# Encoder step on one core: the sample's small matmuls and the score products laid out over all 128 rows

## The chip, the cores and the metric

One Trainium2 chip, one of its cores. The metric is device microseconds (us) of one execution. TensorE (PE in the profile, its weight loads PEld) multiplies, VectorE (DVE), ScalarE (ACT) and GpSimd (POOL) do the elementwise work, SyncE (SP) issues most DMAs.

## The reference

One inference step of a two-layer encoder for two groups of tokens: a prompt of 512 positions and a sample of 32 with 256 cached positions. What matters here of each layer:

```python
# mixing: q, k, v, u, gv = split(rmsnorm(x) @ w_in)
s = einsum('bqhmd,bkhmd->bhmqk', q, k) * (DA_DK ** -0.5)      # 4 heads, 2 maps of 64
s = where(chunk-causal mask, s, NEG);  p = softmax(s)
a = p[:, :, 0] - lam * p[:, :, 1]
o = einsum('bhqk,bkhd->bqhd', a, v)                           # then rmsnorm, (1 - lam_init)
g_out = u * (tril(w_s) @ gv + b_s)                            # 4 groups of 128
x = x + concat(o, g_out) @ w_out
# cross-attention: 4 heads of 256 into 256 memory tokens
x = x + cross_attend(rmsnorm(x), mem_k, mem_v)
# feed-forward of 2816 with a causal convolution of width 3
x = x + conv_ffn(rmsnorm(x))
```

For the sample, k and v are the cached 256 positions and the 32 new ones. New keys, values, gate rows and convolution states are outputs too.

## The kernel before

Activations stand feature by token: x is [128, 8, 544], tokens 0 to 511 the prompt and 512 to 543 the sample. For accuracy an operand is split into a high part of type fp32r and the rest, also fp32r, and a product is three matmuls (high x high, high x low, low x high). Every weight unit is loaded (line 131), split by ScalarE (134) and VectorE (135) and used by the projections of lines 262 and 279 to 281. These are nearly all of TensorE's work.

The rest are small products, and their operands have fewer than 128 rows (partitions) in many places:

- kq_T (427) transposes a head's keys and queries (435), two maps of 64 features one above the other. For map m the own half of kT holds the high part of k, the other half its low part, and qT has the high part of q in both halves, so line 522 computes q_high x (k_high + k_low) over 128 rows. The low part of q times the high part of k is line 524, with the 64 rows of the map's own half: ql[MP[m]] and kT[MP[m], m]. do_attn (509) runs it for four query blocks and two maps per head.
- The sample's keys and queries zs have 32 rows and are transposed at 452. do_attn_sample (548) makes its scores at 554 with a stationary operand of 64 columns (two maps of 32 queries), its transposed difference of probabilities at 565 with 64 rows, and the sum with the cached and the new values at 571 and 572.
- do_gate (636) multiplies the sample's gate rows, 32 of them, at 655. x_stats (219) spreads the 32 scales of the sample at 251. do_cross_scores (809) transposes the sample's 32 rows of probabilities at 860. At the start the sample's input is transposed at 993.

sum_s (300) makes each zs: ScalarE copies one half of a PSUM tile (303), VectorE adds the other (304). Its buffers turn over with two per tag, and zs, gzs and xes share one tag.

The program is written as a stream for one core; the framework's scheduler sets the order on each engine from its own costs when the program is built, and that order is fixed at run time. Engines wait for one another on semaphores. A plain fp32 product shows as two matmuls in the trace, an fp32r one or a transpose as one.

Of the kernel before, what the change touches and what calls it, by code (L numbers as in the profile page):

```python
# [34 lines left out]
def encoder_step(ctx: ExitStack, tc: tile.TileContext, a, o):  # L35
# [183 lines left out]
    def x_stats(need_bc):  # L219
# [20 lines left out]
        dg = G("t4", [128, 4, 128], "dg")  # L240
        dgs = tiny([32, 32], "dgs")
        for t in range(4):
            vec.tensor_scalar(out=dg[:, t], in0=ident, scalar1=r[:, t:t + 1], scalar2=None, op0=ALU.mult)
        vec.tensor_scalar(out=dgs, in0=ident[0:32, 0:32], scalar1=r[0:32, 4:5], scalar2=None, op0=ALU.mult)
        rbc = cp.tile([128, T], F32, tag="rbc", name="rbc")
        for i in range(2):
            pb = psS("pbc")
            for t in range(2):
                pe.matmul(out=pb[:, 128 * t:128 * t + 128], lhsT=ones, rhs=dg[:, 2 * i + t], start=True, stop=True)
            if i == 1:  # L250
                pe.matmul(out=pb[:, 256:288], lhsT=ones[0:32], rhs=dgs, start=True, stop=True)
            act.copy(rbc[:, 256 * i:256 * i + 256 + 32 * i], pb[:, 0:256 + 32 * i])  # L252
# [47 lines left out]
    def sum_s(ps, name):  # L300
        zt = tmp([32, 256], "zt", tag="zs1", bufs=1)
        zs = tmp([32, 256], name, tag="vs" if name == "vs" else "zs", bufs=2)
        act.copy(zt, ps[32:64, 0:256])
        vec.tensor_tensor(out=zs, in0=ps[0:32, 0:256], in1=zt, op=ALU.add)  # L304
        return zs
# [4 lines left out]
    def load_consts(l):  # L310
# [52 lines left out]
        vec.tensor_scalar(out=c["nlam"], in0=c["nlam"], scalar1=-lam_init, scalar2=None, op0=ALU.add)  # L363
        c["eye"] = cp.tile([64, 32], F32, tag="eye", name="eye")
        pool.tensor_copy(c["eye"][0:32], ident[0:32, 0:32])
# [36 lines left out]
    def do_kq(l, h, ve):  # L402
        c = LC[l]
        pr, pv, prs = proj_tm(pop(f"kq{h}"))
        z = G("zr", [128, 4, 256], "z")
        sq = G("t4", [128, 4, 256], "sq")
        for i in range(2):
            act.copy(z[:, 2 * i:2 * i + 2], pv[i])
            act.activation(out=sq[:, 2 * i:2 * i + 2], in_=pv[i], func=AF.Square)
        zs = sum_s(prs, "zs")  # L410
        sqs = tmp([32, 256], "sqs", tag="zs1", bufs=1)
        act.activation(out=sqs, in_=zs, func=AF.Square)
# [9 lines left out]
        norm_rope(zs.unsqueeze(1), 32, 1, None, rs[0:32, 16:20], c, 4)  # L422
        sp.dma_start(out=o["dkp"][l, 0, :, h].rearrange("(t p) m d -> p t (m d)", p=128), in_=z[:, :, 0:128])
        sp.dma_start(out=o["dks"][l, 0, :, h].rearrange("p m d -> p (m d)"), in_=zs[:, 0:128])
        return z, zs

    def kq_T(l, h, z, zs):

        kT = G("kq", [128, 2, 512], "kT", F32R)
        qT = G("kq", [128, 2, 512], "qT", F32R)  # L430
        ql = G("p", [128, 512], "ql", F32R)
        for half in range(2):
# [3 lines left out]
            for m in range(2):  # L436
# [4 lines left out]
                else:  # L441
                    act.activation(out=qT[own, m], in_=ps[own], func=AF.Copy, scale=0.125)
                    vec.scalar_tensor_tensor(out=ql[own], in0=ps[own], scalar=0.125, in1=f32(qT[own, m]),
                                             op0=ALU.mult, op1=ALU.subtract)
# [6 lines left out]
        for half in range(2):  # L451
            pe.transpose(ps[:, 256 + 32 * half:288 + 32 * half], zs[:, 128 * half:128 * half + 128],
                         ident[0:32, 0:32])
        skq = tmp([128, 352], "skq", tag="skq", bufs=2)
        act.copy(skq[:, 0:288], ps[:, 0:288])
        for m in range(2):
            pr = slice(64 * m, 64 * m + 64)
            pool.memset(skq[pr, 320 - 32 * m:352 - 32 * m], 0.0)
            act.activation(out=skq[pr, 288 + 32 * m:320 + 32 * m], in_=ps[pr, 288:320], func=AF.Copy, scale=0.125)
        return kT, qT, ql, skq  # L460

    def do_v(l, hp, r):
# [4 lines left out]
        zs = sum_s(prs, "vs")  # L467
        vec.tensor_scalar(out=zs, in0=zs, scalar1=r[0:32, 4:5], scalar2=None, op0=ALU.mult)
        hv = 2 * hp
        sp.dma_start(out=o["dvp"][l, 0, :, hv:hv + 2].rearrange("(t p) h d -> p t (h d)", p=128), in_=vr)  # L470
        sp.dma_start(out=o["dvs"][l, 0, :, hv:hv + 2].rearrange("p h d -> p (h d)"), in_=zs)
        return [(vr[:, :, 128 * j:128 * j + 128], zs[:, 128 * j:128 * j + 128]) for j in range(2)]

# [35 lines left out]
    def do_attn(l, h, kqs, vv, og):  # L509
# [6 lines left out]
        for i in range(4):  # L516
# [6 lines left out]
            for m in range(2):  # L523
                pe.matmul(out=ps[m][:, 0:nn], lhsT=ql[MP[m], q0:q0 + 128], rhs=kT[MP[m], m, 0:nn],
                          start=False, stop=True)
                vec.memset(ps[m][0:64, n - 64:n], NEG)
# [21 lines left out]
    def do_attn_sample(l, h, kqs, vv, st):  # L548
# [4 lines left out]
        ps = psS("pSs")  # L553
        pe.matmul(out=ps[0:64, 0:288], lhsT=skq[:, 288:352], rhs=skq[:, 0:288], start=True, stop=True)
        e = G("e", [64, 320], "es")
        mx = tiny([64, 4], "mxs")
        vec.tensor_reduce(out=mx[:, 0:1], in_=ps[0:64, 0:288], axis=AX, op=ALU.max, negate=True)
        act.activation(out=e[:, 0:288], in_=ps[0:64, 0:288], func=AF.Exp, bias=mx[:, 0:1], accum_out=mx[:, 1:2])
        vec.reciprocal(out=mx[:, 2:3], in_=mx[:, 1:2])
# [43 lines left out]
    def do_gv(l, j, r):  # L603
# [7 lines left out]
        zs = sum_s(prs, "gzs")  # L611
        vec.tensor_scalar(out=zs, in0=zs, scalar1=r[0:32, 4:5], scalar2=None, op0=ALU.mult)
# [4 lines left out]
        gelu2(zs, t1s)  # L617
        z8 = z.rearrange("p t (g c) -> p (t g) c", c=128)
        zs2 = zs.rearrange("p (g c) -> p g c", c=128)
        for b in range(8):  # L620
# [10 lines left out]
        vec.tensor_tensor(out=t1s.rearrange("p (g c) -> p g c", c=128), in0=zs.rearrange("p (g c) -> p g c", c=128),  # L631
                          in1=c["gmg"][0:32].unsqueeze(1).to_broadcast([32, 2, 128]), op=ALU.mult)
# [3 lines left out]
    def do_gate(l, j, vn, zs, ws):  # L636
# [172 lines left out]
    def do_cross_scores(h, mk, cmT, qq):  # L809
# [38 lines left out]
        for dc in range(2):  # L848
            pe.matmul(out=ps[0:32, 0:256], lhsT=qs[:, dc], rhs=cmT[:, dc], start=(dc == 0), stop=(dc == 1))
        es = tmp([32, 256], "xes", tag="zs", bufs=2)  # L850
        sx = tiny([32, 4], "sxs")
        vec.tensor_reduce(out=sx[:, 0:1], in_=ps[0:32, 0:256], axis=AX, op=ALU.max)
        vec.tensor_tensor(out=sx[:, 1:2], in0=sx[:, 0:1], in1=nrq[0:32, 4:5], op=ALU.mult)
        act.activation(out=es, in_=ps[0:32, 0:256], func=AF.Exp, scale=rq[0:32, 4:5], bias=sx[:, 1:2],
                       accum_out=sx[:, 2:3])
        vec.reciprocal(out=sx[:, 3:4], in_=sx[:, 2:3])
        vec.tensor_scalar(out=es, in0=es, scalar1=sx[:, 3:4], scalar2=None, op0=ALU.mult)
        pt = psB("pxsT")
        for mc in range(2):
# [267 lines left out]
```

## Time and profile before

| | |
|---|---|
| median of 3 runs | 1704.07 us (1703.63 to 1704.73) |
| profiled execution | 1704.66 us, its span 1702.9 us |
| TensorE busy | 1683.1 us (99%), 13115 matmuls |
| VectorE, ScalarE, GpSimd busy | 1006.2 (59%), 727.5 (43%), 250.4 (15%) us |
| granted TensorE clock | 1.00 of full speed over nearly all the span |

Busy time of TensorE counts pipelined matmuls whose ends are modelled, so its share says that it has work, not that it runs at its peak; how fast it goes is read from the steps between starts.

### The profile page before, as it was taken

How to read it: one execution, taken by the hardware profiler on the slowest of the kernel's cores; microseconds unless marked ns; L12 is line 12 of the kernel's file. 1: busy time of each engine (PE TensorE's matmuls, PEld its weight loads, DVE VectorE, ACT ScalarE, POOL GpSimd, SP SyncE). 2: the span in 40 equal slices, each digit the busy share in tenths (PEclk: the TensorE clock that was granted, in tenths of full speed). 3: DMA queues.
4: the chain of work that ended last, by engine and by line, in shares of the span. 5: the costliest groups of instructions: out<-in, count | busy, mean ns of one | idle time of the engine just before them, and what ended most of it. 6: DMA issues, size and time to landing. Idle time of an engine off the chain costs nothing.

```text
span 1702.9 us, 32510 instructions
## 1 busy us (share of the span) xinstructions
PE 1683.1 (99%) x13115; PEld 1623.8 (95%) x13115; DVE 1006.2 (59%) x2218; ACT 727.5 (43%) x1481; POOL 250.4 (15%) x676
## 2 busy tenths in 40 slices
PE   7999999999999999999999999999999999999998
PEld 6988899999999999999998888999999999999998
DVE  6778765565476634665367677555555765256642
ACT  5456754454333312333345576545543333133321
POOL 3000014221211000110111000332222110001100
PEclk9999999999999999999999999999999999999999
DMA  6222133442223233223342222243332323333141
GB/s 185 81 87 72 64 103 101 137 131 90 88 75 94 70 87 111 87 69 88 94 121 68 76 70 79 87 131 112 117 95 75 93 64 88 101 93 99 55 119 55
DMA packets 200988, 158.03 MB, mean 93 GB/s; under 512 B 8670, under 2 KB 200038, under 8 KB 200838
## 3 DMA queue, kind: packets, MB, share of 16 engines
q1 hardware_dynamic: 200774, 155.82, 30.0%
q8 instruction: 103, 1.69, 0.4%
q14 instruction: 47, 0.39, 0.1%
q10 hardware_dynamic: 64, 0.14, 0.0%
HBM read 144.83 MB, written 11.10 MB: 92 GB/s over the span
## 4 chain that ended last, share of the span: by engine, by line
PE 95%; ACT 1%; DVE 1%; SPq 1%; POOL 1%; DMA 0%; issue 0%; ACTq 0%
PE pfda L262 8%; PE pfua L262 8%; PE pfga L262 8%; PE pfdb L262 8%; PE pfub L262 8%; PE pfgb L262 8%; PE pr L281 4%; PE pr L279 4%; PE pr L280 4%; PE pwob L262 3%; PE pwoa L262 3%; PE pwca L262 3%; PE pqb L262 3%; PE pqa L262 3%; PE pwcb L262 3%; PE pm L281 2%
## 5 line engine op out<-in xcount | busy, mean ns | idle before, releaser
L135 DVE TENSOR_TENSOR hl<-raw,hl 128x1024 fp32r<-128x1024 f32 (+2 forms) x280 | 316.6, 1132 | 256.7 <-ACT hl L134 256.1
L134 ACT CAST hl<-raw 128x1024 fp32r<-128x1024 f32 (+2 forms) x280 | 269.9, 964 | 403.5 <-PE pfdb L262 137.6
L262 PE MATMUL pfda<-at,hl 128*128 128x272 f32 x1056 | 266.6, 289 | 0.0
L262 PE MATMUL pfdb<-at,hl 128*128 128x272 f32 x1056 | 266.3, 288 | 0.0
L262 PE MATMUL pfga<-hx,hl 128*128 128x272 f32 x1056 | 263.8, 287 | 0.0
L262 PE MATMUL pfgb<-hx,hl 128*128 128x272 f32 x1056 | 263.7, 287 | 0.0
L262 PE MATMUL pfua<-hx,hl 128*128 128x272 f32 x1056 | 259.3, 287 | 0.5 <-ACT rbc L252 0.5
L262 PE MATMUL pfub<-hx,hl 128*128 128x272 f32 x1056 | 259.1, 287 | 0.0
L262 PEld LDWEIGHTS pfda<-at,hl 128*128 128x128 f32 x1056 | 199.2, 189 | 0.0
L262 PEld LDWEIGHTS pfdb<-at,hl 128*128 128x128 f32 x1056 | 198.7, 188 | 0.1
L262 PEld LDWEIGHTS pfga<-hx,hl 128*128 128x128 f32 x1056 | 198.5, 188 | 0.0
L262 PEld LDWEIGHTS pfgb<-hx,hl 128*128 128x128 f32 x1056 | 198.4, 188 | 0.0
L262 PEld LDWEIGHTS pfua<-hx,hl 128*128 128x128 f32 x1056 | 196.2, 188 | 0.7 <-ACT rbc L252 0.7
L262 PEld LDWEIGHTS pfub<-hx,hl 128*128 128x128 f32 x1056 | 196.2, 188 | 0.0
L280 PE MATMUL pr<-hl,hx 128*128 128x256 f32 x512 | 147.0, 288 | 2.7 <-DVE hl L135 2.7
L279 PE MATMUL pr<-hl,hx 128*128 128x256 f32 x512 | 146.8, 287 | 1.4 <-DVE vs L304 0.9
L281 PE MATMUL pr<-hl,hx 128*128 128x256 f32 x512 | 147.7, 289 | 0.1
L280 PEld LDWEIGHTS pr<-hl,hx 128*128 128x128 f32 x512 | 97.1, 190 | 5.7 <-DVE hl L135 3.2
L279 PEld LDWEIGHTS pr<-hl,hx 128*128 128x128 f32 x512 | 98.0, 192 | 4.0 <-DVE vs L304 1.1
L281 PEld LDWEIGHTS pr<-hl,hx 128*128 128x128 f32 x512 | 96.9, 190 | 3.3 <-issue 1.4
L262 PE MATMUL pwcb<-co,hl 128*128 128x272 f32 x384 | 87.1, 288 | 0.0
L262 PE MATMUL pwca<-co,hl 128*128 128x272 f32 x384 | 86.9, 289 | 0.0
(358 smaller groups left out, 3330.0 us busy)
## 6 DMA issues: line engine op xcount, KB each, us to landing
raw<-in_w_up_dram SPq DMA_DIRECT2D x80, 512.0 KB
raw<-in_w_down_dram SPq DMA_DIRECT2D x32, 512.0 KB
raw<-in_w_in_dram SPq DMA_DIRECT2D x24, 512.0 KB
raw<-in_w_in_dram SPq DMA_DIRECT2D x32, 256.0 KB
raw<-in_w_out_dram SPq DMA_DIRECT2D x32, 256.0 KB
raw<-in_wq_c_dram SPq DMA_DIRECT2D x16, 512.0 KB
raw<-in_wk_c_dram SPq DMA_DIRECT2D x16, 512.0 KB
raw<-in_wv_c_dram SPq DMA_DIRECT2D x16, 512.0 KB
```

The source lines that it names most:

```text
L134: act.copy(hl[:, 0, 0:n * wc], raw[:, 0:n * wc])
L135: vec.tensor_tensor(out=hl[:, 1, 0:n * wc], in0=raw[:, 0:n * wc], in1=f32(hl[:, 0, 0:n * wc]), op=ALU.subtract)
L262: pe.matmul(out=ps[0 if n0 == 0 else 1][:, 0:nn], lhsT=hl[:, wpart, kk, col * 128:col * 128 + 128], rhs=mv[:, n0:n0 + nn], start=first and ...
L279: pe.matmul(out=out, lhsT=lh(k), rhs=hl[:, 0, k % 4], start=(k == 0), stop=False)
L280: pe.matmul(out=out, lhsT=lh(k), rhs=hl[:, 1, k % 4], start=False, stop=False)
L281: pe.matmul(out=out, lhsT=ll(k), rhs=hl[:, 0, k % 4], start=False, stop=(k == k8 - 1))
```

## The change

Every small product named above, except those of lines 571, 572, 582 and the narrow statistics, gets operands of 128 rows, with zeros where there was nothing:

- ql becomes [128, 2, 512]; the half that isn't the map's own is set to zero by GpSimd, and line 524 multiplies all 128 rows.
- zs, gzs, vs and xes become [128, 256] tiles that GpSimd sets to zero before their first 32 rows are written; their transposes and products take all 128 rows, and a transpose writes 128 columns where it wrote 32.
- skq puts the queries first, and line 554 takes columns 0 to 127 as its stationary operand: 64 columns of queries and 64 of cached keys, whose scores nobody reads. The softmax of the sample runs over 128 partitions. eye is zero below row 64, so line 565 multiplies 128 rows, of which 64 count.
- dgs and the input tile xins get 128 rows; xins is set to zero by VectorE before its DMA.

```diff
-        dgs = tiny([32, 32], "dgs")
+        dgs = tiny([128, 32], "dgs")
...
-                pe.matmul(out=pb[:, 256:288], lhsT=ones[0:32], rhs=dgs, start=True, stop=True)
+                pe.matmul(out=pb[:, 256:288], lhsT=ones, rhs=dgs, start=True, stop=True)
...
-        zs = tmp([32, 256], name, tag="vs" if name == "vs" else "zs", bufs=2)
+        zs = tmp([128, 256], name, tag="vs" if name == "vs" else "zs", bufs=2)
+        pool.memset(zs, 0.0)
         act.copy(zt, ps[32:64, 0:256])
-        vec.tensor_tensor(out=zs, in0=ps[0:32, 0:256], in1=zt, op=ALU.add)
+        vec.tensor_tensor(out=zs[0:32], in0=ps[0:32, 0:256], in1=zt, op=ALU.add)
...
-        c["eye"] = cp.tile([64, 32], F32, tag="eye", name="eye")
+        c["eye"] = cp.tile([128, 32], F32, tag="eye", name="eye")
+        pool.memset(c["eye"], 0.0)
...
-        ql = G("p", [128, 512], "ql", F32R)
+        ql = G("p", [128, 2, 512], "ql", F32R)
+        for m in range(2):
+            pool.memset(f32(ql[MP[1 - m], m]), 0.0)
...
-            pe.transpose(ps[:, 256 + 32 * half:288 + 32 * half], zs[:, 128 * half:128 * half + 128],
-                         ident[0:32, 0:32])
+            pe.transpose(ps[:, 256 + 128 * half:384 + 128 * half], zs[:, 128 * half:128 * half + 128], ident)
...
-                pe.matmul(out=ps[m][:, 0:nn], lhsT=ql[MP[m], q0:q0 + 128], rhs=kT[MP[m], m, 0:nn],
+                pe.matmul(out=ps[m][:, 0:nn], lhsT=ql[:, m, q0:q0 + 128], rhs=kT[:, m, 0:nn],
                           start=False, stop=True)
...
-        pe.matmul(out=ps[0:64, 0:288], lhsT=skq[:, 288:352], rhs=skq[:, 0:288], start=True, stop=True)
-        e = G("e", [64, 320], "es")
+        pe.matmul(out=ps[:, 0:288], lhsT=skq[:, 0:128], rhs=skq[:, 64:352], start=True, stop=True)
+        e = G("e", [128, 320], "es")
...
-            pe.matmul(out=pgs[:, 32 * jj:32 * jj + 32], lhsT=zs[:, 128 * jj:128 * jj + 128], rhs=ws[0:32, g, 0:32],
+            pe.matmul(out=pgs[:, 32 * jj:32 * jj + 32], lhsT=zs[:, 128 * jj:128 * jj + 128], rhs=ws[:, g, 0:32],
...
-        es = tmp([32, 256], "xes", tag="zs", bufs=2)
+        es = tmp([128, 256], "xes", tag="zs", bufs=2)
+        pool.memset(es, 0.0)
...
-            pe.transpose(pt[:, 32 * mc:32 * mc + 32], es[:, 128 * mc:128 * mc + 128], ident[0:32, 0:32])
+            pe.transpose(pt[:, 128 * mc:128 * mc + 128], es[:, 128 * mc:128 * mc + 128], ident)
...
-    xs = G("zr", [32, 1024], "xins")
-    act.dma_start(out=xs, in_=a["x_sample"][0])
+    xs = G("zr", [128, 1024], "xins")
+    vec.memset(xs, 0.0)
+    act.dma_start(out=xs[0:32], in_=a["x_sample"][0])
...
-        pe.transpose(ps[1][:, 256:288], xs[:, 128 * kt:128 * kt + 128], ident[0:32, 0:32])
+        pe.transpose(ps[1][:, 256:384], xs[:, 128 * kt:128 * kt + 128], ident)
```

How the built order stands, first on TensorE at the transposes of head 0 in layer 0 (ptr are the prompt's, ptrs the cached keys' and the sample's). Before:

```order
L296 MATMUL prs<-hl,xsm 64x256 x16
L435 MATMUL ptr<-ident,z 128x128 x8
L450 MATMUL ptrs<-ident,ck 128x128 x2
L452 MATMUL ptrs<-ident,zs 128x32 x2
L279 MATMUL pr<-hl,hx 128x256
```

Now:

```order
L296 MATMUL prs<-hl,xsm 64x256 x16
L439 MATMUL ptr<-ident,z 128x128 x8
L454 MATMUL ptrs<-ident,ck 128x128 x2
L456 MATMUL ptrs<-ident,zs 128x128 x2
L279 MATMUL pr<-hl,hx 128x256
```

The sequence is the same (line numbers are a few higher), and the sample's transposes write 128 columns. On TensorE at the first scores of head 0 (pS are the scores, pr the projection of a later head). Before:

```order
L279 MATMUL pr<-hl,hx 128x256
L522 MATMUL pS<-kT,qT 128x256
L524 MATMUL pS<-kT,ql 128x256
L280 MATMUL pr<-hl,hx 128x256
L281 MATMUL pr<-hl,hx 128x256
```

Now:

```order
L281 MATMUL pr<-hl,hx 128x256
L525 MATMUL pS<-kT,qT 128x256
L279 MATMUL pr<-hl,hx 128x256
L527 MATMUL pS<-kT,ql 128x256
L280 MATMUL pr<-hl,hx 128x256
```

One projection matmul now stands between the two score products; elsewhere the kinds of matmuls follow each other as before but for a few neighbours. On GpSimd at the copies that make qT of head 0 (s are the sums of a softmax). Before:

```order
L458 MEMSET skq 64x32
L458 MEMSET skq 64x32 [waits Pool_49]
L445 CAST qT<-qT 64x512 [waits Activation_49] x2
L529 COPY s_682<-sm 128x1 [waits Activation_49,Pool_49]
L529 COPY s_682<-sm 128x1 [waits Activation_49] x2
```

Now:

```order
L461 MEMSET skq 64x32
L461 MEMSET skq 64x32 [waits Pool_49]
L449 CAST qT<-qT 64x512 [waits Activation_49]
L303 MEMSET zs 128x256 [waits DVE_49,DMAHW5_49,PE_49,Pool_49]
L449 CAST qT<-qT 64x512 [waits Activation_49]
L532 COPY s_688<-sm 128x1 [waits Activation_49,Pool_49]
```

The memset of a later zs stands between the two copies and waits for VectorE, TensorE and a DMA. GpSimd has 42 memsets more than before in all.

## Rows read from the trace of the kernel before

**Rows 1.** The page's busy times: us, share of the span, instructions.
```profile
PE 1683.1 (99%) x13115; PEld 1623.8 (95%) x13115; DVE 1006.2 (59%) x2218; ACT 727.5 (43%) x1481; POOL 250.4 (15%) x676
```
**Rows 2.** The chain that ended last, shares of the span by engine.
```profile
PE 95%; ACT 1%; DVE 1%; SPq 1%; POOL 1%; DMA 0%; issue 0%; ACTq 0%
```
**Rows 3.** TensorE's waits: waiting <- waited for: us in total, times, longest.
```profile
PE pxina L991 <- DMA xin<-in_x_prompt_dram: 5.8, 1, 5.8
PE pr L280 <- DVE hl L135: 2.7, 2, 2.4
PE pxsT L860 <- DVE pT L175: 1.3, 2, 0.7
PE pwob L262 <- DVE s L647: 1.2, 2, 0.6
```
**Rows 4.** Groups by form on TensorE: count, busy us, mean ns, idle before.
```profile
L822 PE MATMUL pxS<-mkT,xq 128*128 128x256 f32 x192 | 28.9, 288 | 0.0
...
L524 PE MATMUL pS<-kT,ql 64*128 64x256 f32 x32 | 12.2, 381 | 0.0
```
**Rows 5.** Timeline of TensorE, a score product: start us, us, instruction.
```profile
62.33 0.28 PE L281 MATMUL pr<-hl,hx 128*128 128x256 f32 x1
62.45 0.28 PE L522 MATMUL pS<-kT,qT 128*128 128x256 f32 x1
62.66 0.38 PE L524 MATMUL pS<-kT,ql 64*128 64x256 f32 x1
62.98 0.39 PE L279 MATMUL pr<-hl,hx 128*128 128x256 f32 x1
63.20 0.28 PE L280 MATMUL pr<-hl,hx 128*128 128x256 f32 x1
```
**Rows 6.** Timeline of TensorE, two score products side by side.
```profile
189.16 0.62 PE L522 MATMUL pS<-kT,qT 128*128 128x384 f32 x2
189.71 0.44 PE L524 MATMUL pS<-kT,ql 64*128 64x384 f32 x2
190.08 0.68 PE L296 MATMUL prs<-hl,xsm 128*64 128x256 f32 x4
```
**Rows 7.** Timeline of TensorE, the sample's probabilities between transposes.
```profile
107.88 0.27 PE L543 MATMUL poT<-ident,ot 128*128 128x128 f32 x1
108.09 0.40 PE L565 MATMUL paTs<-es 64*128 64x32 f32 x2
108.42 0.33 PE L543 MATMUL poT<-ident,ot 128*128 128x128 f32 x1
```
**Rows 8.** Timeline of TensorE, the sample's scores.
```profile
84.56 0.28 PE L279 MATMUL pr<-hl,hx 128*128 128x256 f32 x1
84.77 0.70 PE L554 MATMUL pSs<-skq 128*64 128x288 f32 x2
85.40 0.39 PE L280 MATMUL pr<-hl,hx 128*128 128x256 f32 x1
```
**Rows 9.** Timeline of TensorE, the sample's transposes.
```profile
110.85 0.38 PE L450 MATMUL ptrs<-ident,ck 128*128 128x128 f32 x2
111.16 0.30 PE L452 MATMUL ptrs<-ident,zs 32*128 32x32 f32 x2
111.40 0.44 PE L522 MATMUL pS<-kT,qT 128*128 128x384 f32 x1
```
**Rows 10.** Timeline of SyncE, GpSimd and TensorE before head 0's first scores.
```profile
52.49 1.05 SPq L424 DMA_DIRECT2D out_dks_dram<-zs  x1
...
55.12 0.68 POOL L445 CAST qT<-qT 64x512 fp32r<-64x512 f32 x1 [10.90 <-ACT qT L442]
58.08 0.61 POOL L445 CAST qT<-qT 64x512 fp32r<-64x512 f32 x1 [2.27 <-ACT qT L442]
...
59.11 0.28 PE L522 MATMUL pS<-kT,qT 128*128 128x256 f32 x1
```
**Rows 11.** Groups by form on VectorE: count, busy us, mean ns, idle before.
```profile
L74 DVE MEMSET ones<- 128x128 f32 x1 | 0.2, 165 | 0.9 <-PEq L1114 0.9
```

More of the change, by code (lines that the diff above doesn't have):

```diff
@@ L240, in x_stats @@
         dg = G("t4", [128, 4, 128], "dg")
-        dgs = tiny([32, 32], "dgs")
+        dgs = tiny([128, 32], "dgs")
         for t in range(4):
             vec.tensor_scalar(out=dg[:, t], in0=ident, scalar1=r[:, t:t + 1], scalar2=None, op0=ALU.mult)
-        vec.tensor_scalar(out=dgs, in0=ident[0:32, 0:32], scalar1=r[0:32, 4:5], scalar2=None, op0=ALU.mult)
+        vec.tensor_scalar(out=dgs, in0=ident[:, 0:32], scalar1=r[:, 4:5], scalar2=None, op0=ALU.mult)
         rbc = cp.tile([128, T], F32, tag="rbc", name="rbc")
@@ L411, in do_kq @@
         sqs = tmp([32, 256], "sqs", tag="zs1", bufs=1)
-        act.activation(out=sqs, in_=zs, func=AF.Square)
+        act.activation(out=sqs, in_=zs[0:32], func=AF.Square)
         ss = tiny([128, 20], "ss")
@@ L421, in do_kq @@
         norm_rope(z, 128, 4, None, rs[:, 0:16], c, 0)
-        norm_rope(zs.unsqueeze(1), 32, 1, None, rs[0:32, 16:20], c, 4)
+        norm_rope(zs[0:32].unsqueeze(1), 32, 1, None, rs[0:32, 16:20], c, 4)
         sp.dma_start(out=o["dkp"][l, 0, :, h].rearrange("(t p) m d -> p t (m d)", p=128), in_=z[:, :, 0:128])
-        sp.dma_start(out=o["dks"][l, 0, :, h].rearrange("p m d -> p (m d)"), in_=zs[:, 0:128])
+        sp.dma_start(out=o["dks"][l, 0, :, h].rearrange("p m d -> p (m d)"), in_=zs[0:32, 0:128])
         return z, zs
@@ L442, in kq_T @@
                     act.activation(out=qT[own, m], in_=ps[own], func=AF.Copy, scale=0.125)
-                    vec.scalar_tensor_tensor(out=ql[own], in0=ps[own], scalar=0.125, in1=f32(qT[own, m]),
+                    vec.scalar_tensor_tensor(out=ql[own, m], in0=ps[own], scalar=0.125, in1=f32(qT[own, m]),
                                              op0=ALU.mult, op1=ALU.subtract)
@@ L451, in kq_T @@
         for half in range(2):
-            pe.transpose(ps[:, 256 + 32 * half:288 + 32 * half], zs[:, 128 * half:128 * half + 128],
-                         ident[0:32, 0:32])
+            pe.transpose(ps[:, 256 + 128 * half:384 + 128 * half], zs[:, 128 * half:128 * half + 128], ident)
         skq = tmp([128, 352], "skq", tag="skq", bufs=2)
-        act.copy(skq[:, 0:288], ps[:, 0:288])
+        act.copy(skq[:, 64:352], ps[:, 0:288])
         for m in range(2):
             pr = slice(64 * m, 64 * m + 64)
-            pool.memset(skq[pr, 320 - 32 * m:352 - 32 * m], 0.0)
-            act.activation(out=skq[pr, 288 + 32 * m:320 + 32 * m], in_=ps[pr, 288:320], func=AF.Copy, scale=0.125)
+            pool.memset(skq[pr, 32 - 32 * m:64 - 32 * m], 0.0)
+            act.activation(out=skq[pr, 32 * m:32 + 32 * m], in_=ps[pr, 384:416], func=AF.Copy, scale=0.125)
         return kT, qT, ql, skq
@@ L467, in do_v @@
         zs = sum_s(prs, "vs")
-        vec.tensor_scalar(out=zs, in0=zs, scalar1=r[0:32, 4:5], scalar2=None, op0=ALU.mult)
+        vec.tensor_scalar(out=zs[0:32], in0=zs[0:32], scalar1=r[0:32, 4:5], scalar2=None, op0=ALU.mult)
         hv = 2 * hp
         sp.dma_start(out=o["dvp"][l, 0, :, hv:hv + 2].rearrange("(t p) h d -> p t (h d)", p=128), in_=vr)
-        sp.dma_start(out=o["dvs"][l, 0, :, hv:hv + 2].rearrange("p h d -> p (h d)"), in_=zs)
-        return [(vr[:, :, 128 * j:128 * j + 128], zs[:, 128 * j:128 * j + 128]) for j in range(2)]
+        sp.dma_start(out=o["dvs"][l, 0, :, hv:hv + 2].rearrange("p h d -> p (h d)"), in_=zs[0:32])
+        return [(vr[:, :, 128 * j:128 * j + 128], zs[0:32, 128 * j:128 * j + 128]) for j in range(2)]
     def softmax_diff(ps, p, n, e, c, name):
@@ L553, in do_attn_sample @@
         ps = psS("pSs")
-        pe.matmul(out=ps[0:64, 0:288], lhsT=skq[:, 288:352], rhs=skq[:, 0:288], start=True, stop=True)
-        e = G("e", [64, 320], "es")
-        mx = tiny([64, 4], "mxs")
-        vec.tensor_reduce(out=mx[:, 0:1], in_=ps[0:64, 0:288], axis=AX, op=ALU.max, negate=True)
-        act.activation(out=e[:, 0:288], in_=ps[0:64, 0:288], func=AF.Exp, bias=mx[:, 0:1], accum_out=mx[:, 1:2])
+        pe.matmul(out=ps[:, 0:288], lhsT=skq[:, 0:128], rhs=skq[:, 64:352], start=True, stop=True)
+        e = G("e", [128, 320], "es")
+        mx = tiny([128, 4], "mxs")
+        vec.tensor_reduce(out=mx[:, 0:1], in_=ps[:, 0:288], axis=AX, op=ALU.max, negate=True)
+        act.activation(out=e[:, 0:288], in_=ps[:, 0:288], func=AF.Exp, bias=mx[:, 0:1], accum_out=mx[:, 1:2])
         vec.reciprocal(out=mx[:, 2:3], in_=mx[:, 1:2])
@@ L611, in do_gv @@
         zs = sum_s(prs, "gzs")
-        vec.tensor_scalar(out=zs, in0=zs, scalar1=r[0:32, 4:5], scalar2=None, op0=ALU.mult)
+        vec.tensor_scalar(out=zs[0:32], in0=zs[0:32], scalar1=r[0:32, 4:5], scalar2=None, op0=ALU.mult)
         t1s = tmp([32, 256], "gts", tag="zs1", bufs=1)
@@ L616, in do_gv @@
         gelu2(z, t1)
-        gelu2(zs, t1s)
+        gelu2(zs[0:32], t1s)
         z8 = z.rearrange("p t (g c) -> p (t g) c", c=128)
-        zs2 = zs.rearrange("p (g c) -> p g c", c=128)
+        zs2 = zs[0:32].rearrange("p (g c) -> p g c", c=128)
         for b in range(8):
@@ L630, in do_gv @@
         vec.tensor_tensor(out=zs2, in0=zs2, in1=rs[0:32, 8:10].unsqueeze(2).to_broadcast([32, 2, 128]), op=ALU.mult)
-        vec.tensor_tensor(out=t1s.rearrange("p (g c) -> p g c", c=128), in0=zs.rearrange("p (g c) -> p g c", c=128),
+        vec.tensor_tensor(out=t1s.rearrange("p (g c) -> p g c", c=128), in0=zs2,
                           in1=c["gmg"][0:32].unsqueeze(1).to_broadcast([32, 2, 128]), op=ALU.mult)
@@ L853, in do_cross_scores @@
         vec.tensor_tensor(out=sx[:, 1:2], in0=sx[:, 0:1], in1=nrq[0:32, 4:5], op=ALU.mult)
-        act.activation(out=es, in_=ps[0:32, 0:256], func=AF.Exp, scale=rq[0:32, 4:5], bias=sx[:, 1:2],
+        act.activation(out=es[0:32], in_=ps[0:32, 0:256], func=AF.Exp, scale=rq[0:32, 4:5], bias=sx[:, 1:2],
                        accum_out=sx[:, 2:3])
         vec.reciprocal(out=sx[:, 3:4], in_=sx[:, 2:3])
-        vec.tensor_scalar(out=es, in0=es, scalar1=sx[:, 3:4], scalar2=None, op0=ALU.mult)
+        vec.tensor_scalar(out=es[0:32], in0=es[0:32], scalar1=sx[:, 3:4], scalar2=None, op0=ALU.mult)
         pt = psB("pxsT")
         for mc in range(2):
-            pe.transpose(pt[:, 32 * mc:32 * mc + 32], es[:, 128 * mc:128 * mc + 128], ident[0:32, 0:32])
+            pe.transpose(pt[:, 128 * mc:128 * mc + 128], es[:, 128 * mc:128 * mc + 128], ident)
         pTs = tmp([128, 2, 32], "pTs", tag="aTs", bufs=1)
-        vec.tensor_copy(pTs, pt[:, 0:64].rearrange("p (m t) -> p m t", m=2))
+        vec.tensor_copy(pTs, pt[:, 0:256].rearrange("p (m t) -> p m t", m=2)[:, :, 0:32])
         return pT, pTs
```

## The prediction

> **What bounds the kernel.** I read the busy times first, then TensorE's waits, then the timeline of TensorE around the matmuls that the change touches, where the step from one start to the next counts and not the modelled duration. TensorE is busy 99% of the span and every other engine below 60% [rows 1], and 95% of the chain that ended last is TensorE's [rows 2]. What it waits for by name is little: 5.8 us for the first input, 2.7 for weights in the first 30 us, some 1 us each at a handful of other places [rows 3]. So a step that TensorE saves is time saved, unless the saving only brings it earlier to one of these waits.
>
> The steps show where TensorE loses time without waiting for anybody. In a plain stream a 256-column matmul starts 0.12 us after the one before (62.33 to 62.45 in [rows 5]). Around the score matmul of line 524, whose operands have 64 rows, it doesn't: 0.21 us from the L522 ahead to L524, 0.32 from L524 to the next, 0.22 to the one after, 0.75 for three steps where 0.36 is usual. The excess is **0.39 us for one matmul**. The stretched steps lie at the change from 128 rows to 64 and back. A control supports that it is the row count: line 822 also issues 256-column products that add low parts into the same sum, with 128 rows, and its 192 matmuls take 0.288 us each where the 32 of L524 take 0.381 [rows 4].
>
> **The change, part by part.** TensorE keeps its number of instructions and, by the order shown above, its sequence but for a few neighbours; what changes is the shape of eight kinds of them. I price each by the excess steps that disappear.
>
> Scores (L524): two layers of four heads, four query blocks and two maps make 64. On the timeline 54 stand alone among 128-row matmuls: 54 x 0.39 = 21.1 us. Four stand in two adjacent pairs, where the two maps use different halves of the rows; from the first L522 at 189.16 to the matmul behind the pair at 190.08 are 0.92 us for four 384-column steps [rows 6], and at 0.12 x 384/256 = 0.18 a step these need 0.72, so 0.20 a pair, 0.4 in all. The other six stand within two steps of another narrow matmul, which keeps part of the excess (lines 571 and 572 stay narrow): I take 0.25 each, 1.5. Together **23.0 us**, between 19 (0.30 each) and 25 (0.39 for all 64). I use 0.39 at 512 columns too, because the entry and the exit are what is lost, not the columns. The Trainium skill, "TensorE: Matmul & The Clock Gate", section "LDWEIGHTS (loading the stationary operand)", has the load's time go with the columns and not with the rows; by that alone the full-row form would be no cheaper, this term 0 and the sum below 7.9. The rows show the steps, not the loads, and the steps are stretched.
>
> Sample's probabilities (L565, eight groups of three): the first of a group comes 0.21 us after a transpose and the transpose behind its two passes 0.33 later, 0.54 for one block [rows 7]; with full rows I expect a transpose and two passes at 0.11 each, 0.33. Two such blocks save 0.42 to 0.5; the third writes 32 columns and stays narrow, so I give it nothing. In the last head of each layer the three stand together with one entry and one exit: a quarter of that, 0.15, is my estimate. So 6 x 0.5 + 2 x 0.15 = **3.3 us**.
>
> Sample's scores (L554, eight, of two passes): 0.21 to the first pass and 0.63 for both with the exit [rows 8], and the next step stretched by 0.10 as in [rows 5]. Entry 0.09, exit about 0.1, next step 0.10: 0.3 each, **2.4 us**. How long a 288-column pass with all columns of the array takes isn't in the trace; the two here take about 0.27 each without the exit, and I take no change; 0.05 a pass either way would be 0.8 in all.
>
> Transposes of the sample (L452 and L860, 16 pairs): 0.20 us from the last L450 (110.96) to the first L452, 0.24 for the two, then L522 [rows 9]. Three full transposes at 0.11 would need 0.33 instead of 0.44, and the next step loses its 0.10: 0.2 a pair, 3.3 if all counts. About half of the pairs stand where TensorE then waits for VectorE ([rows 3] has pxsT among them), and there the saving goes into the wait: I take **2.0 us**, between 0.9 and 3.3.
>
> Gate and broadcast products of the sample (L655 and L251, eight groups): one entry, one exit, one late next step, 0.28 each by the pattern above: **2.2 us**.
>
> Transposes of the sample's input (L993): eight, all at the very start, and behind them TensorE stands 2.4 us at a stretch until VectorE has the first weights [rows 3]. I take **nothing**, at most 2 us.
>
> What is added: 42 memsets on GpSimd. A copy of 64x512 takes 0.68 us there [rows 10], a memset of that size hardly more, so 16 for ql, 24 of 256 columns at half of that and two small ones are some 19 us on an engine that is busy 15% [rows 1]: nothing, as long as none waits ahead of something urgent (a rival below). On VectorE one memset of 128x1024; 128x128 took 0.165 us [rows 11], so about 1.3, ahead of the sample's input DMA, whose data TensorE first uses behind its first wait of 5.8 us [rows 3]: nothing, at worst 1 us. The wider vector operations (128 partitions for 64) keep their element count per partition, which I price at nothing.
>
> Given back: near the end of each layer's mixing TensorE already waits for the gate and the last head ([rows 3], pwob on line 647's result). What it gains just before, two of L524, one L554, a group of L565 and two of L655, arrives early at the same wait. I take back 1 us a layer, **2.0** in all, between 0 and 4.
>
> Sum: 23.0 + 3.3 + 2.4 + 2.0 + 2.2 - 2.0 = **30.9 us** off the profiled execution's 1704.66 us, 1673.8; that execution lay 0.6 us above the median of the runs, so I forecast **1673 us**. With all lower values (19, 2.5, 1.6, 0.9, 1.5, less 4 and less 1) the gain is 20.5, with all upper ones (25, 3.6, 3.2, 3.3, 2.7, nothing given back) 38.
>
> **Rivals.** *Other engines take half of it back.* With TensorE some 15 us faster per mixing stage, softmax, transposition and evacuation may set the pace at the places where the schedule is tight. Against it: outside the start the waits of [rows 3] are near 1 us in total per place. For it: VectorE is the second busiest engine, 59% over the span, and the score tiles have two buffers, one for each map. Half of the score term lost and another 2 us: 30.9 - 11.5 - 2 = 17 gained, 1687 us. Chance 0.10.
>
> *Nothing is gained.* By the Trainium skill, "TensorE: Matmul & The Clock Gate", section "Why this matters for your kernels", a single matmul with K=32 takes the same time as one with K=128 and the gain of small K lies in running several at once, so padding rows buys nothing and gives up the chance of overlap. As a mechanism of this kernel: the late steps would belong to the place and not to the row count, and stay; the small pair price of [rows 6] is what overlap looks like. That would be 1704 us. [Rows 4, 5] speak against it. Chance 0.04.
>
> *Slower, by GpSimd's order.* In the new order the memset of a later zs stands between the two copies that make qT of head 0, and it waits for the output DMA of the earlier zs, among others. That DMA was issued at 52.49 to 53.54 and the copies ran at 55.12 and 58.08, with 2.27 us free between them; the first scores follow at 59.11, 0.42 us after the second copy's end [rows 10]. If the DMA lands after 58, the copy, the scores and TensorE wait. Such a wait decides from 33/8 = 4.1 us a head on; at 5 us for each of eight heads the kernel would take 1704 - 33 + 40 = 1711 us. In the other heads the memsets stand ahead of both copies or wait for matmuls issued long before. Chance 0.03.
>
> **How the numbers follow.** The forecast, a gain of 20 to 38 us, has 0.83. The range runs from 1666 (all upper bounds) to 1686 (a gain of 18, most of the first rival's side), which leaves out less than 2 in 10. A difference of 0.2% is 3.4 us, about what runs of this kernel can tell from none: faster 0.93 (forecast and first rival), same 0.04 (nothing gained), slower 0.03 (GpSimd's order).
>
> **What would show it.** In the changed profile the step into and out of the low-part scores should be 0.12 us at 256 columns and the group's mean duration near 0.288 instead of 0.381; L565's first two blocks 0.33 instead of 0.54; the pairs of sample transposes 0.11 a step. TensorE's busy share stays at 99% in a span shorter by 30 us, and the savings lie in the two mixing stages, about 14 us each, hardly any in the feed-forward stages. I am wrong if those steps stay stretched, or if TensorE's list of waits grows by more than 5 us.

## The result and the profile after

| | before | after |
|---|---|---|
| median of 4 runs | 1704.13 us (1703.63 to 1704.73) | 1672.08 us (1671.94 to 1672.29) |
| span of the profiled execution | 1702.9 us | 1670.4 us |

The ratio is 0.9814, 95% interval [0.9802, 0.9825]: 32 us faster, against 1673.0 us forecast and a range of 1666 to 1686. First the page's busy times and the chain by engine, beside [rows 1, 2] (line numbers are up to six higher now):

```profile
PE 1647.6 (99%) x13115; PEld 1619.0 (97%) x13115; DVE 1006.9 (60%) x2219; ACT 725.4 (43%) x1481; POOL 267.1 (16%) x718
...
PE 94%; DVE 2%; ACT 2%; issue 1%; POOL 1%; DMA 0%; ACTq 0%
```

The same 13115 matmuls still fill 99% of a span that is 32.5 us shorter, and TensorE's busy time fell by 35.5 us. GpSimd has 16.7 us more. The groups by form, beside [rows 4], show the second score product at the duration of any other 256-column product:

```profile
L826 PE MATMUL pxS<-mkT,xq 128*128 128x256 f32 x192 | 28.9, 288 | 0.0
...
L527 PE MATMUL pS<-kT,ql 128*128 128x256 f32 x32 | 9.0, 281 | 0.0
```

On TensorE's timeline round the first of them (compare [rows 5]) every step is 0.12 us, into L527 (59.20 to 59.32), out of it (59.44) and on (59.55):

```profile
59.08 0.28 PE L525 MATMUL pS<-kT,qT 128*128 128x256 f32 x1
59.20 0.28 PE L279 MATMUL pr<-hl,hx 128*128 128x256 f32 x1
59.32 0.28 PE L527 MATMUL pS<-kT,ql 128*128 128x256 f32 x1
59.44 0.28 PE L280 MATMUL pr<-hl,hx 128*128 128x256 f32 x1
59.55 0.28 PE L281 MATMUL pr<-hl,hx 128*128 128x256 f32 x1
...
81.59 0.28 PE L279 MATMUL pr<-hl,hx 128*128 128x256 f32 x1
81.71 0.65 PE L558 MATMUL pSs<-skq 128*128 128x288 f32 x2
81.97 0.49 PE L280 MATMUL pr<-hl,hx 128*128 128x256 f32 x1
...
103.16 0.31 PE L569 MATMUL paTs<-es 128*128 128x32 f32 x2
103.30 0.31 PE L546 MATMUL poT<-ident,ot 128*128 128x128 f32 x1
103.45 0.31 PE L569 MATMUL paTs<-es 128*128 128x32 f32 x2
...
105.40 0.38 PE L454 MATMUL ptrs<-ident,ck 128*128 128x128 f32 x2
105.62 0.38 PE L456 MATMUL ptrs<-ident,zs 128*128 128x128 f32 x2
105.76 0.42 PE L525 MATMUL pS<-kT,qT 128*128 128x384 f32 x1
```

The sample's scores (81.59 to 81.97) take 0.38 us where [rows 8] have 0.84; when several passes stand together, the last step of a group reads short and the one behind it long, so groups are compared with two steps behind them. The probabilities take 0.29 us from one block to the next, with a transpose between them; the transposes of the sample start 0.11 us apart. TensorE's list of waits, all rows of at least 0.8 us, beside [rows 3]:

```profile
PE pxina L997 <- DMA xin<-in_x_prompt_dram: 4.8, 1, 4.8
PE pr L280 <- DVE hl L135: 1.8, 1, 1.8
PE pxinb L999 <- DMA xins<-in_x_sample_dram: 1.5, 1, 1.5
PE pr L281 <- DVE hx L191: 1.4, 2, 1.1
PE pxsT L865 <- DVE pT L175: 1.3, 2, 0.7
PE pxinb L997 <- DVE x L1001: 1.3, 1, 1.3
PE pwob L262 <- DVE s L651: 1.2, 2, 0.6
PE pr L279 <- DVE vs L305: 0.9, 2, 0.5
PE pfua L262 <- ACT rbc L252: 0.8, 2, 0.4
PE pr L279 <- ACT x L1000: 0.8, 1, 0.8
```

The waits inside the layers (pxsT, pwob) are what they were. New are those at the input's transposes (L999 and L997), 2.8 us in the first 17 us, and those for hx (1.4) and x (0.8) behind them. The whole list grew by some 3 us, less than the 5 that the prediction named as a sign of being wrong.

Where the time went, from the start of the same matmul in the two traces:

| point in the program | before | after | difference, us |
|---|---|---|---|
| first input transpose | 5.84 | 4.82 | -1.02 |
| first projection | 16.57 | 16.94 | +0.37 |
| transposes of head 3, layer 0 | 152.98 | 142.81 | -10.17 |
| first memory transpose (mixing is over) | 268.23 | 252.53 | -15.70 |
| first down projection | 594.34 | 578.20 | -16.14 |
| first transpose of head 0, layer 1 | 887.98 | 871.55 | -16.43 |
| first memory transpose, layer 1 | 1103.41 | 1071.29 | -32.12 |
| last output transposes | 1691.51 | 1658.97 | -32.54 |

Counted from the first projection, mixing gives 16.1 us in layer 0 and 15.7 in layer 1, and what stands behind each mixing 0.7 and 0.4. The input loses: from the first transpose to the first projection TensorE takes 12.1 us where it took 10.7. That the first transpose comes 1.0 us earlier isn't shown to be the change's doing: in the twelve kept traces it starts anywhere between 4.62 and 5.84 us.

### The profile page after: what moved, and what is told of

The parts are those of the page before. It is cut to its first block, busy times and chain, and to the rows that moved or that the text cites. A ratio compares the mean times of both kernels' runs of the same rounds, so it can differ in the third digit from the quotient of the medians.

```text
span 1670.4 us, 32582 instructions
## 1 busy us (share of the span) xinstructions
PE 1647.6 (99%) x13115; PEld 1619.0 (97%) x13115; DVE 1006.9 (60%) x2219; ACT 725.4 (43%) x1481; POOL 267.1 (16%) x718
## 4 chain that ended last, share of the span: by engine, by line
PE 94%; DVE 2%; ACT 2%; issue 1%; POOL 1%; DMA 0%; ACTq 0%
PE pfda L262 8%; PE pfua L262 8%; PE pfga L262 8%; PE pfdb L262 8%; PE pfub L262 8%; PE pfgb L262 8%; PE pr L279 3%; PE pr L281 3%; PE pr L280 3%; PE pwob L262 3%; PE pwoa L262 3%; PE pwca L262 3%; PE pqb L262 3%; PE pqa L262 3%; PE pwcb L262 3%; PE pm L281 2%
## 5 line engine op out<-in xcount | busy, mean ns | idle before, releaser
L135 DVE TENSOR_TENSOR hl<-raw,hl 128x1024 fp32r<-128x1024 f32 (+2 forms) x280 | 315.3, 1127 | 253.9 <-ACT hl L134 253.5
```

The lines of the kernel that those rows point to most:

```text
L135: vec.tensor_tensor(out=hl[:, 1, 0:n * wc], in0=raw[:, 0:n * wc], in1=f32(hl[:, 0, 0:n * wc]), op=ALU.subtract)
```

## The experiments

The theory: TensorE loses about 0.38 us in its steps round each group of matmuls that use fewer rows than their neighbours, for the way in and the way out together, and no other engine has a part in it. The rivals: the late steps belong to the place and not to the rows; other engines take part of a gain back; GpSimd's memsets are in the way.

**Scores alone.** The kernel before with this part of the change:

```diff
-        ql = G("p", [128, 512], "ql", F32R)
+        ql = G("p", [128, 2, 512], "ql", F32R)
+        for m in range(2):
+            pool.memset(f32(ql[MP[1 - m], m]), 0.0)
...
-                pe.matmul(out=ps[m][:, 0:nn], lhsT=ql[MP[m], q0:q0 + 128], rhs=kT[MP[m], m, 0:nn],
+                pe.matmul(out=ps[m][:, 0:nn], lhsT=ql[:, m, q0:q0 + 128], rhs=kT[:, m, 0:nn],
```

> The kernel before with ql and its second score matmuls alone on 128 rows. Theory (each change between a 128-row matmul and a narrower one costs TensorE some 0.38 us in lengthened steps round the narrow group, 54 groups alone and 6 beside narrow ones): 1682 us (1680 to 1684), and the steps round the second score matmuls of 256 columns 0.12 us each. Rival (the lengthened steps belong to the place in the program, to buffers or releases there, not to the rows): 1704 us. Rival (other engines take half back): 1693.

Measured: 1681.43 us against 1703.96, ratio 0.9869 [0.9853, 0.9886], a gain of 22.5 us. TensorE's instructions stand in the same order in both traces, so the steps can be compared one by one: those at the 64 products got 22.9 us shorter, all others together 0.1. By form, with 128 rows in place of 64:

```profile
L526 PE MATMUL pS<-kT,ql 128*128 128x256 f32 x32 | 9.0, 280 | 0.0
```

**All but the scores.** The reverse edit, in the changed kernel.

> The changed kernel with the second score matmuls back on 64 rows, all its other parts kept. Theory: the 22 us of the scores come back and the rest stays: 1694 us (1692 to 1696). Rival (the gains of the parts overlap, so that either part alone gives most): below 1690. Rival (the other parts gain nothing): 1704.

Measured: 1694.58 us, 22.5 more than the changed kernel. With 64 rows the group is back at its old mean, by form:

```profile
L525 PE MATMUL pS<-kT,ql 64*128 64x256 f32 x32 | 12.2, 381 | 0.0
```

The same 22.5 us come and go with the rows at the same place in the same order: not the place, and no overlap with the other parts.

**The sample's scores and probabilities alone**, in the kernel before (eye of 128 rows, queries first in skq, ps and es of 128 rows).

> The kernel before with the sample's scores (128 columns of weights) and its probabilities' product (128 rows) alone changed. Theory: 2.4 + 3.3 us by the prediction, 2.7 + 3.5 by the steps left over in the trace: 1698 us (1697 to 1699.5). Rival (the sample's chain waits for the other engines, which have as much to do as before): 1703 or more.

Measured: 1697.33 us, 6.6 less than before. The steps at line 554 lost 2.7 us and those at 565 4.0.

**The sample's rows alone**, in the kernel before (zs, gzs, vs, xes and dgs of 128 rows with their memsets).

> The kernel before with only the sample's 32 rows filled up to 128 with zeros (transposes of keys and queries, gate, the broadcast of 1/rms, transposes of the cross-attention's probabilities); scores, the sample's scores and probabilities and the input's transposes as before. Theory: 2.0 + 2.2 us by the prediction: 1700 us (1698.5 to 1701.5). Rival (GpSimd's memsets of 128x256 hold the small sums up and the waits take it back): 1703 to 1706.

Measured: 1700.46 us, ratio 0.9979 [0.9970, 0.9989], 3.5 less. Steps: 0.9 at the transposes of keys and queries, 0.8 at those of the probabilities, 1.2 at the gate, 0.6 at the broadcast. The parts add up: 22.5 + 6.6 + 3.5 = 32.6 us for a change that gave 32.0. The 0.6 between them isn't clear of noise: the kernel before alone had medians from 1703.96 to 1704.47 us beside these runs. In none of the parts are the transposes of the sample's input.

**That input's memset on rows 32 to 127 only.** In the changed kernel TensorE waits 1.5 us for the load of the sample. VectorE's and ScalarE's queues at the start of that trace show why: the load is issued when the memset is done, at 2.17 us, where before it was at 1.5 us.

```profile
1.23 0.91 DVE L983 MEMSET xins<- 128x1024 f32 x1 [0.16 <-issue]
...
2.17 0.33 ACTq L984 DMA_DIRECT2D xins<-in_x_sample_dram  x1
```

```diff
-    vec.memset(xs, 0.0)
+    vec.memset(xs[32:64], 0.0)
+    vec.memset(xs[64:128], 0.0)
```

> The changed kernel with the memset of the sample's input on rows 32 to 127 only, so that the load of the sample need not wait for it. Theory (the new waits at the input's transposes, 1.5 us on the load, are this memset's): 1671 us (1670.4 to 1671.8). Rival (the load is late for another reason, or another wait ends as late): 1672.1.

Measured: 1670.61 us, 1.5 less than the changed kernel and within the range expected. The load is issued at 1.5 us again, and no wait for it is left in TensorE's list. From the first matmul to the first transpose of head 0 TensorE takes 46.5 us before, 47.6 in the changed kernel and 45.4 here. So without the late load this stretch is 1.1 us shorter than before: 0.3 to 0.4 at the broadcast (line 251), which lies in it, and some 0.7 for the input's transposes on full rows.

Whether those 0.7 us come of the rows alone isn't shown, as TensorE's speed changes in this stretch. Before, one full transpose of the input follows another after 0.21 us to the end; a step of 0.11 us appears at 13.4 us in the changed kernel and at 9.5 us here. Then, behind the waits round the first projections, products of 256 columns step at 0.21 us again until about 23 us, and the granted clock reads 0.50 there, the lower of its two levels (1.2 GHz): at 20 to 22 us in the changed kernel, at 17 to 23 here. The kernel before has the same slow steps up to 23 us, though its record of the granted clock reads 1.00.

**The first score products on 64 rows too**, in the kernel before. This tells a price for each change from a price for each narrow matmul:

```diff
-                pe.matmul(out=ps[m][:, 0:nn], lhsT=qT[:, m, q0:q0 + 128], rhs=kT[:, m, 0:nn], start=True, stop=False)
+                pe.matmul(out=ps[m][:, 0:nn], lhsT=qT[MP[m], m, q0:q0 + 128], rhs=kT[MP[m], m, 0:nn], start=True, stop=False)
```

> The kernel before with the first score matmuls on 64 rows too (each map's own half; this leaves out the product of the query's high part with the key's low part). The four matmuls of a tile are then all narrow. Theory (the price is for the change of rows: once in, once out): no further loss, 1704 us (1702 to 1707). Rival (each narrow matmul pays for itself, or the change between the upper and the lower 64 rows does): 32 tiles with two more narrow matmuls, 0.38 us a tile more or about 12 us, 1716; at 0.38 for each of 64, 1728.

Measured: 1707.06 us against 1704.47, ratio 1.0015 [1.0006, 1.0025]: 2.6 more, 0.06 beyond the theory's range and far from the rival's 12. The scheduler had put the products in another order: 72 narrow groups (50 pairs, 20 single ones, 2 of four) where there were 62. TensorE's timeline has both kinds:

```profile
61.90 0.28 PE L281 MATMUL pr<-hl,hx 128*128 128x256 f32 x1
62.10 0.38 PE L524 MATMUL pS<-kT,ql 64*128 64x256 f32 x1
62.41 0.38 PE L279 MATMUL pr<-hl,hx 128*128 128x256 f32 x1
62.63 0.28 PE L280 MATMUL pr<-hl,hx 128*128 128x256 f32 x1
...
66.23 0.28 PE L281 MATMUL pr<-hl,hx 128*128 128x256 f32 x1
66.44 0.38 PE L522 MATMUL pS<-kT,qT 64*128 64x256 f32 x1
66.66 0.28 PE L524 MATMUL pS<-kT,ql 64*128 64x256 f32 x1
66.87 0.39 PE L279 MATMUL pr<-hl,hx 128*128 128x256 f32 x1
67.10 0.28 PE L280 MATMUL pr<-hl,hx 128*128 128x256 f32 x1
```

From 61.90 to 62.63 a single one takes 0.73 us for three steps, 0.37 over the usual 0.36. From 66.23 to 67.10 a pair takes 0.87 us for four, 0.39 over the usual 0.48. A second narrow matmul in a group costs nothing more, and all groups at 256 columns with nothing narrow near them agree: 0.39 us for each of 16 single ones and 20 pairs. Ten more groups would be 3.9 us if all stood alone.

By the Trainium skill, "TensorEngine Tiling (Array Packing)", section "Key Properties", TensorE is drained when the tiling mode changes. The stretched steps on the way into and out of the 64 rows fit that, at 0.39 us for the two changes together; that the mode is what changes isn't seen in a trace.

**Where a narrow operand begins.** In the changed kernel, map 0 takes 96 rows:

```diff
-                pe.matmul(out=ps[m][:, 0:nn], lhsT=ql[:, m, q0:q0 + 128], rhs=kT[:, m, 0:nn],
+                rr = slice(0, 96) if m == 0 else slice(0, 128)
+                pe.matmul(out=ps[m][:, 0:nn], lhsT=ql[rr, m, q0:q0 + 128], rhs=kT[rr, m, 0:nn],
```

> The changed kernel with the second score matmuls of map 0 on rows 0 to 95 (64 of data, 32 of zeros), those of map 1 on all 128. Theory A (what counts is whether the operand goes beyond 64 rows; the transposes of 124 rows at line 334 aren't stretched): 1672 us (1671.5 to 1673.5). Theory B (any operand below 128 rows pays the change): 32 changes of 0.385 us, 12.3 in all: 1684 us (1682 to 1685).

Measured: 1672.02 us, no difference. By form:

```profile
L528 PE MATMUL pS<-kT,ql 96*128 96x256 f32 x16 | 4.5, 284 | 0.0
L528 PE MATMUL pS<-kT,ql 128*128 128x256 f32 x16 | 4.5, 282 | 0.0
```

So 96 rows count as full and 64 don't; what lies between wasn't tried.

**GpSimd's memsets four times.** Each of the 40 memsets of ql, zs, vs, gzs and xes in the changed kernel was issued four times:

```diff
-            pool.memset(f32(ql[MP[1 - m], m]), 0.0)
+            for _ in range(4):
+                pool.memset(f32(ql[MP[1 - m], m]), 0.0)
```

> The changed kernel with each added memset of GpSimd in the layers (query's low part, sample's rows, cross-attention's probabilities) issued four times. Theory (GpSimd has room, nothing late hangs on these): 1672 us (1671.8 to 1673). Rival of the prediction (the memsets stand between GpSimd's copies that the scores need): 1675 to 1690, with TensorE's waits for qT or ql grown.

Measured: 1678.42 us (1677.11 to 1679.81), 6.3 more than the changed kernel, so the theory's "nothing" doesn't hold for this run. But it isn't the rival's wait in each head: in the profiled execution (1677.32) 5.2 us are lost before the first head's transposes, which start at 57.56 instead of 52.40, and from there to the last matmul both traces take 1613.6 us. Why two of the four executions took some 2.4 us longer than this one isn't known. The scheduler had set many of the memsets at the very start, ahead of most of GpSimd's sums of squares, but TensorE's two new waits are for other things:

```profile
PE ptr L441 <- DVE zs L403: 2.2, 1, 2.2
...
PE pws L604 <- POOL ws L600: 1.9, 1, 1.9
```

GpSimd's mask of ws at L600 waits for its load, which SyncE issues at 36.61 us instead of 31.52, behind more weight loads. L403 on VectorE stands behind the split of a weight unit (L135, at 55.54); in the changed kernel it stood ahead of such a split. So the build ordered other engines anew at the start, and most of the 5.2 us lie at these two places. What four times the memsets cost in an unchanged order the run doesn't tell; in the layers, from the first head on, they cost nothing.

The rival's mechanism is there too. GpSimd's timeline at head 0 of this run:

```profile
59.43 0.61 POOL L451 CAST qT<-qT 64x512 fp32r<-64x512 f32 x1 [10.13 <-ACT qT L448]
...
61.86 0.32 POOL L304 MEMSET zs<- 128x256 f32 x1 [1.50 <-DMA out_dks_dram<-zs]
62.24 0.61 POOL L451 CAST qT<-qT 64x512 fp32r<-64x512 f32 x1
```

The memset of zs between the two copies of qT waits 1.50 us for the output DMA of the earlier zs, but the first scores follow their head's transposes by 6.1 us, less than the 6.7 of the changed kernel. In that kernel the same memset runs at 55.95 without any wait.

**Few columns, and whether the type matters.** In the changed kernel line 296 has weights of 64 columns and isn't stretched (its steps are 0.12), while the sample's scores with 64 columns were before [rows 8]. One is fp32r, the other plain fp32. In the kernel before, skq is made fp32r:

```diff
-        skq = tmp([128, 352], "skq", tag="skq", bufs=2)
+        skq = tmp([128, 352], "skq", tag="skq", bufs=2, dt=F32R)
```

> The kernel before with the sample's keys and queries rounded to fp32r, so that its scores (64 columns of weights, 128 rows) take one pass instead of two plain fp32 passes; the low parts of these operands are left out. Before, the four steps round a group take 0.210 + 0.294 + 0.336 + 0.231 = 1.071 us. Theory A (few columns of an fp32r product cost nothing at the change, as the 64-column products of line 296, whose steps are 0.12): 0.12 + 0.13 + 0.12 = 0.37 us, 0.70 less for each of eight, 5.6 in all: 1698.9 us (1698 to 1700). Theory B (few columns cost like few rows, whatever the type): the 0.38 of a change stay, 0.32 less, 2.5 in all: 1701.9 us (1701 to 1703).

The timeline of TensorE at the same place as [rows 8]:

```profile
84.50 0.28 PE L279 MATMUL pr<-hl,hx 128*128 128x256 f32 x1
84.62 0.29 PE L554 MATMUL pSs<-skq 128*64 128x288 f32 x1
84.75 0.28 PE L280 MATMUL pr<-hl,hx 128*128 128x256 f32 x1
84.87 0.28 PE L281 MATMUL pr<-hl,hx 128*128 128x256 f32 x1
```

The steps are 0.12, 0.13 and 0.12, in all eight groups, as theory A said. The time is not: 1700.94 us (1699.86 to 1702.48), 3.3 less instead of 5.6. In the kept trace, which is of the slowest of the ten executions, TensorE has a new wait, 2.7 us in two times for the gate's operand:

```profile
PE pg L645 <- ACT gz L629: 2.7, 2, 1.3
```

The build had also moved whole groups of matmuls on TensorE, the gate's among them, so whether the wait comes of the time saved or of the new order isn't shown. The time alone lies between A's range and B's and decides nothing; the steps decide for A.

**The rest of the narrow matmuls, widened**, with the input's memset as above:

```diff
-            pe.matmul(out=pt[0:n, 32 * b:32 * b + 32], lhsT=e[:, 128 * b:128 * b + n], rhs=w, start=True, stop=True)
-        aT = tmp([128, 96], "aTs", tag="aTs", bufs=1)
+            pe.matmul(out=pt[:, 32 * b:32 * b + 32], lhsT=e[:, 128 * b:128 * b + 128], rhs=w, start=True, stop=True)
+        aT = tmp([128, 192], "aTs", tag="aTs", bufs=1)
...
-            pe.matmul(out=po[0:32, 0:128], lhsT=aT[:, 32 * b:32 * b + 32], rhs=cv[:, b], start=(b == 0), stop=False)
-        pe.matmul(out=po[0:32, 0:128], lhsT=aT[0:32, 64:96], rhs=vs, start=False, stop=True)
+            pe.matmul(out=po[:, 0:128], lhsT=aT[:, 32 * b:32 * b + 128], rhs=cv[:, b], start=(b == 0), stop=False)
+        pe.matmul(out=po[:, 0:128], lhsT=aT[:, 64:192], rhs=vs, start=False, stop=True)
...
-            pe.matmul(out=ps[0:32, 0:256], lhsT=qs[:, dc], rhs=cmT[:, dc], start=(dc == 0), stop=(dc == 1))
+            pe.matmul(out=ps[:, 0:256], lhsT=qs[:, 32 * dc:32 * dc + 128], rhs=cmT[:, dc], start=(dc == 0), stop=(dc == 1))
```

Stationary operands overlap in one wider tile, so that most of the added columns need no zeros. The transposes of the sample's result (582) take 128 rows of a tile that is cleared once a layer.

> The changed kernel with the memset as in the run before last, and the remaining narrow matmuls of the layers widened with zeros or unused columns too: third block of the sample's probabilities, the sample's values (weights of 32 columns), transposes of the sample's result, the sample's cross-attention scores (weights of 32 columns). Theory (a change to few rows and a change to few columns cost alike, 1.3 + 3.3 + 1.3 + 2.6 us left over in the trace, and 1 at the start): 1663 us (1661 to 1666). Rival (only few rows cost; few columns don't): 1667 to 1669. Rival (the widened work waits for the other engines): 1671 or more.

Measured: **1665.10 us** (1664.83 to 1665.96), ratio to before 0.9770 [0.9756, 0.9785], the fastest of the study: 7.0 less than the changed kernel, 5.5 of them from the widening. By the steps, against the run with the memset mended: 1.9 at the cross-attention scores, whose weights had 32 columns and all 128 rows, 2.1 at the sample's values, about 1.1 at the transposes of its result, 1.0 at the third block. So few columns do cost where the product is plain fp32. All four came out below what was expected. At the cross-attention that is because its passes of 256 columns keep a step of 0.22 us with full columns too, where an fp32r product of that width steps at 0.12; I had counted the difference as loss. Why the others fell short wasn't followed.

## Why the prediction was right

- **Scores**, 23.0 forecast: 22.9 by the steps, 22.5 by the time, in both directions. The 54 that stand alone gave 20.7 us, 0.38 each where I had 0.39 (48 gave 0.39, and six with the 64-column products of line 296 behind them 0.33). The six beside other narrow ones gave 0.31 on average, not 0.25, and the two pairs 0.17 each instead of 0.20, with every step counted once.
- **Sample's probabilities**, 3.3: 4.0. A head saves 0.61, not 0.5, and the last head of a layer 0.19, not 0.15. From the first pass of one block to that of the next, with the transpose between, 0.59 became 0.29, so two blocks give 0.6. I had counted the first from its transpose to the next one ([rows 7], 0.54) and expected 0.33 after; it is 0.25, because the two passes of 32 columns take 0.14 and not 0.22. The third block, still narrow, saves 0.02, as taken.
- **Sample's scores**, 2.4: 2.7, 0.34 a group. Entry, exit and late step are as priced; the first pass takes 0.24 us instead of 0.29, the 0.05 that I had named as possible.
- **Transposes**, 2.0: 1.7. As forecast, half of the pairs gain nothing, because TensorE waits behind them anyway (for VectorE's vs, or at pxsT); the others gain the 0.21 that I had priced.
- **Gate and broadcast**, 2.2: 1.8. The gate's four groups gave 0.31 each. Of the broadcast's four only two gained, 0.3 each; in the other two the wait behind it, for ScalarE's copy (rbc, at pfua), grew from 0.23 to 0.42 us and took the gain. I had priced all eight alike from the pattern of the scores.
- **Input's transposes**, "nothing, at most 2": some 0.7 once the load isn't late. The memset of xins, for which I allowed "at worst 1 us", cost 1.5. It ran 0.91 us instead of the estimated 1.3, but I looked at the wrong cover: the first wait of 5.8 us is for the prompt's data, and the transposes of the sample's input then wait for their own.
- **Given back**, 2.0 at the end of mixing: nothing there. The wait on the gate (pwob) is 1.2 us in both traces, so VectorE's result for it came earlier by as much as TensorE did. This step failed. What was lost is at the start, 1.4 us between the first matmul and the first projection. The five gains above were forecast at 32.9 us in all and came to 33.1 by the steps. That the time then came out within 1 us is in part luck: a loss that I hadn't priced stands in for one that didn't come.
- **Rivals.** "Nothing is gained" fell with the two score runs: the row count decides, at the same place. The Trainium skill's rule that a single matmul of few rows takes as long as one of 128 ("TensorE: Matmul & The Clock Gate", "Why this matters for your kernels") is about the time of one matmul; this kernel lost its time in the steps at the change from one row count to the other. "Other engines take half back" wasn't seen with this change; the fp32r run has such a wait, 2.7 us in two times, but in a changed order. "Slower, by GpSimd's order": its wait never came with 42 memsets, and with four times as many it came once, for 1.50 us, and held nothing up.

## What to carry to other kernels

Read the steps from one start to the next on a TensorE that counts as 99% busy: a narrow matmul among full ones costs here 0.38 us that no list of waits shows, and zeros that fill its rows cost nothing on TensorE. Count groups, not matmuls: keep narrow ones together or widen every one of them. Zeros have a place in the queues too: clear only what the load doesn't write, so that the load needn't wait (1.5 us here).

## What the runs showed that I had not expected

- **Few columns stretch only plain fp32 products.** Weights of 64 columns in fp32r cost nothing (line 296, and the run with skq in fp32r), in plain fp32 they cost 0.34 us a group (64 columns, line 554), and 32 columns up to 0.32 (line 849). A transpose to 32 columns isn't stretched either; in the changed kernel, near the end, two steps together are 0.24 us, the sum of a transpose's 0.11 and a 272-column matmul's 0.125:

```profile
1642.12 0.27 PE L970 MATMUL pyTs<-ident,x 128*32 128x128 f32 x1
1642.14 0.37 PE L262 MATMUL pfdb<-at,hl 128*128 128x272 f32 x1
1642.36 0.29 PE L262 MATMUL pfda<-at,hl 128*128 128x272 f32 x1
```

  For the transpose the Trainium skill, "TensorEngine Tiling (Array Packing)", section "Restrictions", fits: column tiling isn't there for transposes of fp32 or fp32r input. No run shows that this is the reason, and why the fp32r product is spared stays open.
- **Few rows stretch fp32r products, plain fp32 products and transposes alike** (lines 524, 565 and 452): 32 and 64 rows do, 96 don't.
- **Two narrow matmuls on different halves run at once.** The pairs of [rows 6] aren't cheap because they share a change alone: the record of the second starts 3 ns after the first, and the next matmul 0.37 us later, in both layers. By the Trainium skill, "TensorE: Matmul & The Clock Gate", section "Why this matters for your kernels", slices of few rows in distinct row groups run concurrently; the 3 ns between two slices of 64 rows agree. It is the overlap that the "nothing is gained" rival spoke of. The widened pair is still 0.17 us faster, since the two changes cost more than one 384-column step saves.
